# Holding branch a's mask additions in GpSimd's queue until the dilated branch has issued its last addition

## The chip, the cores and the metric

The kernel runs on one core of a Trainium2 chip. The metric is the device time of one execution in microseconds (us), lower is better. The times of the kernel before are the median of three runs.

The engines are named as in the profile: PE (TensorE, matrix products; PEld is its weight loads), DVE (VectorE), ACT (ScalarE), POOL (GpSimd) and SP (SyncE, which only issues transfers here). Each engine works through its own queue of instructions, and the engines wait for each other through semaphores.

## The reference

One decoder layer with 256 tokens and 1024 features. One projection of x feeds three parallel token mixers, whose outputs are gated, merged and normalised; a feed-forward part follows.

```python
proj = x @ w_in[i]
aq, ak, av, iq, ik, iw, bq, bk, bv, cq, ck, cv = jnp.split(proj, SPLIT_POINTS, axis=-1)
o_a = dsa_mixer(...)      # 6 heads: an indexer picks the top 64 keys of each query, softmax over these
o_b = dilated_mixer(...)  # 4 slots, each with 3 query groups of another window and dilation
o_c = moba_mixer(...)     # 6 heads, with 256 tokens: plain causal attention
merged = gates[:, :, 0] * (o_a @ w_br_a) + gates[:, :, 1] * (o_b @ w_br_b) + gates[:, :, 2] * (o_c @ w_br_c)
x = layer_norm(ALPHA * x + merged @ w_out, ln1_g, ln1_b)
h = square(relu(x @ w_up)) @ w_down
x = layer_norm(ALPHA * x + h + sigmoid(x @ w_ple_gate) * (p @ w_ple), ln2_g, ln2_b)
```

Two details matter for the change. In branch b the three query groups of a slot are merged by their softmax denominators; since all three attend to the same keys, this is the sum of their three exponentials divided by the sum of their denominators. In branch a the top-64 choice is a mask that is added to the position bias before the softmax.

## The kernel before

Everything is in fp32. A product is made of three passes on PE, from a high and a low part of each factor (`prod`, lines 133 to 135). So every block of weights that comes from memory (a transfer issued by SP, L71) is split first: ACT casts the high part (`whi`, L75), and the low part (`wlo`, L79) is subtracted by DVE for the first 640 of 1024 columns and by POOL for the rest, up to the 58th block. Five buffers hold raw blocks and five hold split ones. `W.get` splits up to four blocks ahead of the one that PE uses.

The order in each engine's queue is not the order of the program. A planner lays out all queues from its own model of time: among the instructions that are ready in that model it takes the one with the higher priority, mostly the earlier one in the program, so a later instruction that is ready can fill a gap. On the chip each queue then runs in the order that was laid out.

The part around the change, in the program's order:

- **Branch b**, two pairs of slots (`for j in range(2)`, with `slots` for the attention). For each of the two heads of a pair, ACT takes the exponentials of all three groups (L366), POOL adds the second and the third group to the first (L368, then L369, the "query groups" of the change), ACT scales the rows by 1/denominator (`scale_rows`, L333), and in `attend` PE transposes the result (L310 to L312), ACT and DVE split it (L313, L314), and PE multiplies by the values (L317 to L320).
- The features p are loaded and split (`pr`, L466; ACT L467, DVE L468), for use near the end of the layer, and the values of branch c are computed (`values`; copies at L299 and L300).
- **Branch c**, three pairs of heads. The position bias of a head is a tile `T`, loaded by SP from a table in memory (`toeplitz`, L182; three heads to a tile, one transfer each) into one of three buffers.
- **Branch a**, three pairs of heads. The mask `am` (L444) is the result of the top-64 search, a generator called `side` that is advanced step by step from `feat`. For each head n, POOL adds it to the bias tile: `ta = T + am`, in two instructions (L497 for 128 columns, L498 for 256). `ta` has three buffers. DVE reads it in `head` (L341). When the third head of a tile has its `ta`, the buffer of `T` is free for the next tile.

PE works between all of this on gate products (`fill("g")`, results at L238), branch projections (`"c"`, L251) and feature products (`feat`).

An order can be set by hand with `tc.issue_after(ins)`: each instruction traced inside the block on the engine of `ins` is placed behind `ins` in that engine's queue. It is an edge for the planner and adds no semaphore.

Of the kernel before, what the change touches and what calls it, by code (L numbers as in the profile page):

```python
# [13 lines left out]
ALU = mybir.AluOpType  # L14
# [79 lines left out]
def hybrid_layer(ctx: ExitStack, tc: tile.TileContext, x0, xn, pT, wqk, wva, wvb, wg, wbc, wba,  # L94
                 wout, wup, wdq, wdn, wpg, wple, lnrow, rel, onehot, pick, out):
    nc = tc.nc
    pe, act, dve, pool = nc.tensor, nc.scalar, nc.vector, nc.gpsimd
# [69 lines left out]
    for t in TASKS:  # L167
# [4 lines left out]
        elif t in "gcao":  # L172
            u, w, n = {"g": (u_g, wg, 1024), "c": (u_bc, wbc, 640), "a": (u_ba, wba, 768),
                       "o": (u_out, wout, 1024)}[t]
# [4 lines left out]
    def toeplitz(h0, step):  # L179
        t = tp.tile([128, 3, 256], F32, name="T", tag="T")  # L180
        for i in range(3):
            nc.sync.dma_start(t[:, i], bass.AP(  # L182
                tensor=tabd.tensor,
                offset=tabd.offset + (h0 + i * step) * COPIES * N_U + 127,
                ap=[[N_U - 16, 8], [N_U - 1, 16], [1, 256]]))
        return t
# [8 lines left out]
    am = p1.tile([128, 384], F32, name="am")  # L195
# [10 lines left out]
        t = mm.tile([128, 512], F32, name="mm", tag="mm")  # L206
        return t[:, 0:256] if shape == 256 else t

    last = [None]

    def q_pair(ps, scale=-0.125):

        q = qpool.tile([128, 2, S], F32R, name="q", tag="q")
        last[0] = act.mul(q[:, 0], ps, scale).ins
        dve.scalar_tensor_tensor(q[:, 1], ps, scale, q[:, 0].bitcast(F32), op0=ALU.mult,
                                 op1=ALU.subtract)
        return q
# [13 lines left out]
    def fill(what):  # L231


        for w in what:
            if w == "g":
                ps = mmbank(256)
                gemm(ps, u_g[n_g[0]], xs)
                act.activation(G[:, n_g[0]], ps, AF.Tanh, scale=0.5)  # L238
                n_g[0] += 1
                continue  # L240
            f = n_c[0]
            n_c[0] += 1
            hi, lo = W.get(u_bc[f][0])
            ps = mmbank(512).rearrange("p (i s) -> p i s", i=2)
            for i, (k0, k1) in enumerate(((3, 5), (5, 8))):
                for k in range(k0, k1):
                    c = slice((k - 3) * 128, (k - 2) * 128)
                    prod(ps[:, i], (hi[:, c], lo[:, c]), (op[:, k, 0], op[:, k, 1]), k == k0,
                         k == k1 - 1)
            g = G[:, 3 * f + 1:3 * f + 3]  # L250
            dve.scalar_tensor_tensor(g, g, 1.0, ps, op0=ALU.add, op1=ALU.mult)  # L251
            dve.tensor_tensor(g[:, 0], g[:, 0], g[:, 1], op=ALU.add)

    def feat(f):
        ps = mmbank(256)
        gemm(ps, u_q[f], xs)
        if f > 4:
            next(side, None)
        return ps

    def logits(q, k):


        ss = [next(ps_s)[:, 0:384] for _ in range(2)]
        with tc.high_priority(offset=500):
            for b in range(2):
                c = slice(b * 128, (b + 1) * 128)
                for i, (x, y) in enumerate(((1, 0), (0, 0), (0, 1))):
                    for h in (1, 0):
                        d = slice(64 * h, 64 * h + 64)  # L270
                        m = pe.matmul(ss[h][:, QC[b]], lhsT=q[d, x, c],  # L271
                                      rhs=k[d, y, 0:128 * (b + 1)], start=i == 0, stop=i == 2)
                        if b or i or not h:
                            tc.keep_in_program_order(m)
        return ss
# [3 lines left out]
    op = pm.tile([128, 8, 2, S], F32R, name="op")  # L279
# [25 lines left out]
    def attend(P, vh, o, h):  # L305

        hi, lo = pth[n_pt[0] % 2], ptl[n_pt[0] % 2]
        n_pt[0] += 1
        t = next(ps_t)
        pe.transpose(t[:, 0:128], P[:, 256:384], ident)  # L310
        pe.transpose(t[:, 128:256], P[:, 0:128], ident)
        pe.transpose(t[:, 256:384], P[:, 128:256], ident)  # L312
        act.copy(hi[:, 128:512], t[:, 0:384])  # L313
        dve.tensor_tensor(lo[:, 128:512], t[:, 0:384], hi[:, 128:512].bitcast(F32),  # L314
                          op=ALU.subtract)
        v = next(ps_v)
        pe.matmul(v[:, 0:S], lhsT=V[:, 0, vh], rhs=hi[:, 256:512], start=True, stop=False)  # L317
        pe.matmul(v[:, 0:S], lhsT=V[:, 0, vh], rhs=lo[:, 256:512], start=False, stop=False)
        pe.matmul(v[:, 0:S], lhsT=V[:, 1, vh], rhs=hi[:, 0:256], start=False, stop=False)
        pe.matmul(v[:, 0:S], lhsT=V[:, 1, vh], rhs=lo[:, 0:256], start=False, stop=True)  # L320
        x = wk2.tile([64, S], F32, name="ov", tag="ov")
        act.copy(x, v[64:128, 0:S])
        dve.tensor_tensor(o[64 * h:64 * h + 64], v[0:64, 0:S], x, op=ALU.add)

    def pair_out(o, kt):
        act.copy(op[:, kt, 0], o)
        dve.tensor_tensor(op[:, kt, 1], o, op[:, kt, 0].bitcast(F32), op=ALU.subtract)

    def scale_rows(P, den):
        r = sm.tile([128, 2], F32, name="r", tag="r")  # L330
        dve.reciprocal(r, den)
        for b in range(2):
            act.mul(P[:, QC[b]], P[:, QC[b]], r[:, b:b + 1])  # L333


    def head(s, t0, t1, vh, o, h):
        e = wk.tile([128, 384], F32, name="e", tag="e")
        mx = sm.tile([128, 2], F32, name="mx", tag="mx")
        den = sm.tile([128, 2], F32, name="den", tag="den")
        for b, t in enumerate((t0, t1)):  # L340
            dve.tensor_tensor_reduce(e[:, QC[b]], s[h][:, QC[b]], t, op0=ALU.add, op1=ALU.min,  # L341
                                     scale=1.0, scalar=-GONE, accum_out=mx[:, b:b + 1])
        for b in range(2):
            act.activation(e[:, QC[b]], e[:, QC[b]], AF.Exp, bias=mx[:, b:b + 1], scale=-1.0,
                           accum_out=den[:, b:b + 1])
        scale_rows(e, den)
        attend(e, vh, o, h)

    def slots(qs, k, Ts, vh, o):

        es = [wk2.tile([128, 3, 384], F32, name="eb", tag="eb") for _ in range(2)]
        mxs = [sm.tile([128, 2, 3], F32, name="mxb", tag="mxb") for _ in range(2)]
        for g in range(3):
            s = logits(qs[g], k)
            for h in range(2):
                for b, t in enumerate((Ts[h][:, g, 128:256], Ts[h][:, g, :])):
                    dve.tensor_tensor_reduce(es[h][:, g, QC[b]], s[h][:, QC[b]], t, op0=ALU.add,
                                             op1=ALU.min, scale=1.0, scalar=-GONE,
                                             accum_out=mxs[h][:, b, g:g + 1])
        for h in range(2):  # L360
            e = es[h]
            m = sm.tile([128, 2], F32, name="mx", tag="mx")
            den = sm.tile([128, 2], F32, name="den", tag="den")
            dve.tensor_reduce(m, mxs[h], axis=AX.X, op=ALU.min)
            for b in range(2):
                act.activation(e[:, :, QC[b]], e[:, :, QC[b]], AF.Exp, bias=m[:, b:b + 1],  # L366
                               scale=-1.0, accum_out=den[:, b:b + 1])
            pool.tensor_tensor(e[:, 0], e[:, 0], e[:, 1], op=ALU.add)  # L368
            pool.tensor_tensor(e[:, 0], e[:, 0], e[:, 2], op=ALU.add)  # L369
            scale_rows(e[:, 0], den)  # L370
            attend(e[:, 0], vh + h, o, h)

# [15 lines left out]
    with ExitStack() as begin:  # L388
# [4 lines left out]
        with tc.high_priority(offset=1000):  # L393
            for k in range(KT):
                for i, (a, b) in enumerate(cut[k]):
                    e = nc.scalar if i else nc.sync
# [28 lines left out]
    for j in range(4):  # L425
# [3 lines left out]
        for h in range(2):  # L429
            act.activation(r[:, h], s[h], AF.Relu)  # L430
            for b in range(2):
                n = 2 * j + h
# [15 lines left out]
    def opair():  # L448
        return wk2.tile([128, S], F32, name="o", tag="o")
# [21 lines left out]
    for j in range(3):  # L471
# [5 lines left out]
        for h in range(2):  # L477
            n = 2 * j + h
            if n % 3 == 0:
                T = toeplitz(18 + n, 1)  # L480
            head(s, T[:, n % 3, 128:256], T[:, n % 3], 5 + n, o, h)
            fill("g")
        pair_out(o, 5 + j)

    for _ in side:
        pass
    T = None
    for j in range(3):
        q = q_pair(feat(19 + j))
        s = logits(q, kA)  # L490
        o = opair()
        for h in range(2):
            n = 2 * j + h
            if n % 3 == 0:
                T = toeplitz(n, 1)
            ta = wk.tile([128, 384], F32, name="ta", tag="ta")
            pool.tensor_tensor(ta[:, 0:128], T[:, n % 3, 128:256], am[:, 0:128], op=ALU.add)  # L497
            pool.tensor_tensor(ta[:, 128:384], T[:, n % 3], am[:, 128:384], op=ALU.add)  # L498
            head(s, ta[:, 0:128], ta[:, 128:384], 0, o, h)
            fill("gc")  # L500
        pair_out(o, j)
# [436 lines left out]
```

## Time and profile before

| quantity | value |
|---|---|
| time, median of 3 runs | 444.92 us (444.71 to 445.08) |
| time of the profiled execution | 445.0 us |
| its span, first to last instruction | 443.2 us |
| mean granted PE clock | 0.994 of full speed |
| GpSimd's additions for branch b (L368, L369), both pairs | 8 instructions, 8.6 us |
| GpSimd's mask additions (L497, L498) | 12 instructions, 8.3 us |
| GpSimd's weight subtractions (L79) | 58 instructions, 78.5 us |

The span is what the trace covers; the remaining 1.8 us of the execution lie outside it. A row of the timeline gives start, duration, engine, line, operation, output and inputs with their shapes, and in brackets how long the engine had been idle and what ended that wait. Rows of one line that follow each other may be merged (x2, x3). A row of PE's waits gives who waited for whom, the total, the number of times and the longest one. A row of the table by windows gives a stretch of the span and its length, then for PE, PEld, DVE, ACT and POOL the busy time with the number of instructions, the granted clock, the share of the DMA engines and GB/s.

### The profile page before, as it was taken

To read this page: it belongs to the slowest core of one execution; us is meant where nothing else is said; L and a number is where in the kernel's file an instruction comes from. 1 tells how busy PE (TensorE), PEld (TensorE's weight loads), DVE (VectorE), ACT (ScalarE), POOL (GpSimd) and SP (SyncE) were. 2 spreads that over 40 slices of the span, in tenths; PEclk is the share of its full clock that TensorE was granted. 3 is DMA by queue.
4 is the path that set the end of the run, shared out by engine and by line. 5 is a ranking of instruction groups with operands and counts; after the bars stand their busy time and mean duration, and the time that the engine had idled before them with its cause. 6 is when DMAs were issued, how large, how long until landed. Compare 5 with 4: busy or idle time off the path is not lost.

```text
span 443.2 us, 7744 instructions
## 1 busy us (share of the span) xinstructions
PE 429.7 (97%) x2839; PEld 389.3 (88%) x2839; DVE 333.7 (75%) x601; ACT 270.7 (61%) x488; POOL 102.8 (23%) x99
## 2 busy tenths in 40 slices
PE   8999999998999999999999999999999999999992
PEld 8989999998999989999886888888888888888882
DVE  5867977536546568759958769999888978689956
ACT  6765366476877758756604657878877765455500
POOL 2764247378533545500001000000000000000001
PEclk9999999999999999999999999999999999999997
DMA  8895956448635326468870766567655364656502
GB/s 302 298 314 156 286 160 199 150 113 281 224 94 170 126 77 184 131 202 315 260 283 0 248 226 193 190 191 270 204 189 184 100 207 132 228 195 212 215 0 95
DMA packets 27146, 84.28 MB, mean 190 GB/s; under 512 B 2864, under 2 KB 6872, under 8 KB 26724
## 3 DMA queue, kind: packets, MB, share of 16 engines
q1 hardware_dynamic: 25872, 79.54, 54.4%
q10 hardware_dynamic: 1140, 4.19, 2.6%
q8 instruction: 22, 0.36, 0.3%
q14 instruction: 16, 0.13, 0.1%
q0 software_dynamic: 96, 0.06, 0.0%
HBM read 81.88 MB, written 1.90 MB: 189 GB/s over the span
## 4 chain that ended last, share of the span: by engine, by line
PE 89%; DVE 3%; issue 2%; DMA 2%; POOL 2%; ACT 1%; SPq 0%; POOLq 0%; DVEq 0%
PE mm L681 13%; PE mm L133 12%; PE mm L135 12%; PE mm L134 12%; PE b L133 8%; PE b L135 8%; PE b L134 8%; PE mm L683 7%; PE b L271 3%; PE b L409 3%; DMA T<-tabd 1%; DMA pr<-in_pT_dram 1%; PE b L129 1%; DVE st L605 1%; DVE Y L622 1%
## 5 line engine op out<-in xcount | busy, mean ns | idle before, releaser
L75 ACT CAST whi<-raw 128x1024 fp32r<-128x1024 f32 (+3 forms) x147 | 148.0, 1013 | 81.2 <-issue 19.9
L79 DVE TENSOR_TENSOR wlo<-raw,whi 128x1024 fp32r<-128x1024 f32 (+5 forms) x147 | 156.1, 1076 | 42.7 <-ACT whi L75 38.7
L79 POOL TENSOR_TENSOR wlo<-raw,whi 128x384 fp32r<-128x384 f32 (+3 forms) x58 | 78.5, 1359 | 83.2 <-ACT whi L75 74.0
L133 PE MATMUL mm<-xh,whi 128*128 128x256 f32 x336 | 95.0, 283 | 1.0 <-DVE G L251 1.0
L135 PE MATMUL mm<-xh,wlo 128*128 128x256 f32 x336 | 95.6, 285 | 0.0
L134 PE MATMUL mm<-xl,whi 128*128 128x256 f32 x336 | 94.7, 282 | 0.0
L133 PEld LDWEIGHTS mm<-xh,whi 128*128 128x128 f32 x336 | 63.3, 189 | 1.5 <-DVE G L251 1.2
L681 PE MATMUL mm<-x,whi 128*128 128x512 f32 x256 | 64.1, 392 | 0.0
L135 PEld LDWEIGHTS mm<-xh,wlo 128*128 128x128 f32 x336 | 63.3, 188 | 0.8
L134 PEld LDWEIGHTS mm<-xl,whi 128*128 128x128 f32 x336 | 63.3, 188 | 0.3
L612 POOL TENSOR_TENSOR rs<-rs,half 128x1 f32<-128x1 f32 x4 | 4.1, 1028 | 244.5 <-DVE rs L611 244.5
L681 PEld LDWEIGHTS mm<-x,whi 128*128 128x128 f32 x256 | 46.1, 189 | 8.3
L683 PEld LDWEIGHTS mm<-x,wlo 128*128 128x128 f32 x256 | 34.9, 190 | 2.5
L683 PE MATMUL mm<-x,wlo 128*128 128x256 f32 x256 | 35.7, 282 | 0.0
L134 PE MATMUL b<-wlo,hT 128*128 128x512 f32 (+1 forms) x88 | 33.4, 380 | 0.0
L135 PE MATMUL b<-whi,hT 128*128 128x512 f32 (+1 forms) x88 | 33.4, 379 | 0.0
L133 PE MATMUL b<-whi,hT 128*128 128x512 f32 (+1 forms) x88 | 31.9, 379 | 0.0
L686 DVE TENSOR_REDUCE r<-mm 128x256 f32<-128x512 f32 x32 | 22.0, 687 | 6.0 <-PE mm L683 6.0
L742 DVE TENSOR_TENSOR raw<-raw 128x1024 f32<-128x1024 f32 x12 | 14.7, 1222 | 9.0 <-DMA raw<-in_wdq_dram 9.0
L133 PEld LDWEIGHTS b<-whi,hT 128*128 128x128 f32 x88 | 16.6, 188 | 3.1
L135 PEld LDWEIGHTS b<-whi,hT 128*128 128x128 f32 x88 | 16.5, 188 | 3.2
L134 PEld LDWEIGHTS b<-wlo,hT 128*128 128x128 f32 x88 | 16.5, 188 | 3.1
(194 smaller groups left out, 782.0 us busy)
## 6 DMA issues: line engine op xcount, KB each, us to landing
raw<-in_wup_dram SPq DMA_DIRECT2D x32, 512.0 KB
raw<-in_wg_dram SPq DMA_DIRECT2D x24, 512.0 KB
raw<-in_wdn_dram SPq DMA_DIRECT2D x20, 512.0 KB
raw<-in_wqk_dram SPq DMA_DIRECT2D x18, 512.0 KB
raw<-in_wdq_dram SPq DMA_DIRECT2D x12, 512.0 KB
raw<-in_wout_dram SPq DMA_DIRECT2D x8, 512.0 KB
raw<-in_wpg_dram SPq DMA_DIRECT2D x8, 512.0 KB
T<-tabd SPq DMA_DIRECT2D x24, 128.0 KB
```

The lines of the kernel that those rows point to most:

```text
L75: nc.scalar.copy(hi, r)
L79: e.tensor_tensor(lo[:, c], r[:, c], hi[:, c].bitcast(F32), op=ALU.subtract)
L129: pe.transpose(t[:, 0:128], ident, ident)
L133: pe.matmul(ps, lhsT=a[0], rhs=b[0], start=first, stop=False)
L134: pe.matmul(ps, lhsT=a[0], rhs=b[1], start=False, stop=False)
L135: pe.matmul(ps, lhsT=a[1], rhs=b[0], start=False, stop=last)
L271: m = pe.matmul(ss[h][:, QC[b]], lhsT=q[d, x, c], rhs=k[d, y, 0:128 * (b + 1)], start=i == 0, stop=i == 2)
L409: pe.matmul(first[f], lhsT=w[:, k, 128 * f:128 * f + 128], rhs=x[:, k], start=k == i == 0, stop=k == KT - 1 and i == 2)
L681: pe.matmul(ps, lhsT=hi[:, cs[k]], rhs=x1[:, :, k], start=k == 0, stop=False)
L683: pe.matmul(ps[:, :, 0], lhsT=lo[:, cs[k]], rhs=x1[:, :, k, 0], start=False, stop=k == KT - 1)
L686: dve.tensor_reduce(r, ps.rearrange("p b a t -> p b t a"), axis=AX.X, op=ALU.add)
L742: dve.tensor_tensor(t[n], t[x], t[y], op=ALU.subtract)
```

## The change

The last L369 that the program traces (second pair, second head) is remembered, and the mask additions of all six heads of branch a are traced inside an `issue_after` block behind it. `toeplitz`, which loads the bias tiles, and `head`, which reads `ta`, stay outside the block.

```diff
-    last = [None]
+    last, added = [None], [None]
...
             pool.tensor_tensor(e[:, 0], e[:, 0], e[:, 1], op=ALU.add)
-            pool.tensor_tensor(e[:, 0], e[:, 0], e[:, 2], op=ALU.add)
+            added[0] = pool.tensor_tensor(e[:, 0], e[:, 0], e[:, 2], op=ALU.add).ins
...
-    T = None
+    T, held = None, added[0]
...
             ta = wk.tile([128, 384], F32, name="ta", tag="ta")
-            pool.tensor_tensor(ta[:, 0:128], T[:, n % 3, 128:256], am[:, 0:128], op=ALU.add)
-            pool.tensor_tensor(ta[:, 128:384], T[:, n % 3], am[:, 128:384], op=ALU.add)
+            with tc.issue_after(held):
+                pool.tensor_tensor(ta[:, 0:128], T[:, n % 3, 128:256], am[:, 0:128], op=ALU.add)
+                pool.tensor_tensor(ta[:, 128:384], T[:, n % 3], am[:, 128:384], op=ALU.add)
```

The computation is the same. The planner lays out the queues anew with these edges.

## The prediction

> **What bounds the kernel now.** The page comes first: the engine totals.
>
> ```profile
> span 443.2 us, 7744 instructions
> PE 429.7 (97%) x2839; PEld 389.3 (88%) x2839; DVE 333.7 (75%) x601; ACT 270.7 (61%) x488; POOL 102.8 (23%) x99
> ```
>
> PE is busy for all but 13.5 us. A change on POOL, an engine with 23%, can pay only where POOL makes PE wait. So the second view is the list of PE's waits, and the third the table by windows, to place them.
>
> ```profile
> PE b L310 <- POOL wlo L79: 1.4, 1, 1.4
> PE mm L133 <- DVE G L251: 1.0, 1, 1.0
> PE b L310 <- issue: 0.8, 1, 0.8
> ...
> 61.00:73.00 12.00, 12.00 (x108) 11.85 (x107) 7.73 (x16) 9.78 (x21) 9.83 (x9) 1.00 0.50 150
> 82.00:98.00 16.00, 15.32 (x111) 14.86 (x109) 6.16 (x17) 9.25 (x18) 9.26 (x10) 1.00 0.51 149
> 98.00:107.00 9.00, 7.56 (x62) 7.30 (x63) 4.92 (x6) 5.42 (x10) 8.19 (x9) 1.00 0.66 205
> 107.00:150.00 43.00, 43.00 (x377) 42.08 (x377) 25.07 (x66) 32.16 (x79) 20.39 (x14) 1.00 0.53 168
> 150.00:190.00 40.00, 38.98 (x341) 38.10 (x340) 28.82 (x72) 28.41 (x71) 21.15 (x20) 1.00 0.46 139
> ```
>
> After the stretch, PE's busy time and the share of each other engine follow, then the granted clock (1.00 everywhere here). Around the second dilated pair PE loses 16.00 − 15.32 = 0.68 and 9.00 − 7.56 = 1.44 us, 2.12 in all: the two waits before L310, the first transpose of a head's weights. The third wait, 1.0 us, lies in the window from 150 us, after the held additions of the first three heads. Between, PE is gapless.
>
> The fourth view is POOL's timeline around the two waits.
>
> ```profile
> 89.53 1.02 POOL L368 TENSOR_TENSOR eb<-eb 128x384 f32<-128x384 f32 x1
> 92.73 0.47 POOL L497 TENSOR_TENSOR ta<-T,am 128x128 f32<-128x128 f32 x1 [2.19 <-DMA T<-tabd]
> 93.16 1.32 POOL L498 TENSOR_TENSOR ta<-T,am 128x256 f32<-128x256 f32 x1
> 94.44 1.04 POOL L497 TENSOR_TENSOR ta<-T,am 128x128 f32<-128x128 f32 x1
> 95.44 0.73 POOL L498 TENSOR_TENSOR ta<-T,am 128x256 f32<-128x256 f32 x1
> 96.13 1.01 POOL L369 TENSOR_TENSOR eb<-eb 128x384 f32<-128x384 f32 x1
> ...
> 98.06 1.01 POOL L79 TENSOR_TENSOR wlo<-raw,whi 128x384 fp32r<-128x384 f32 x1
> 99.02 0.47 POOL L497 TENSOR_TENSOR ta<-T,am 128x128 f32<-128x128 f32 x1
> 99.45 0.74 POOL L498 TENSOR_TENSOR ta<-T,am 128x256 f32<-128x256 f32 x1
> 100.14 3.16 POOL L79 TENSOR_TENSOR wlo<-raw,whi 128x384 fp32r<-128x384 f32 x2
> 103.27 1.00 POOL L369 TENSOR_TENSOR eb<-eb 128x384 f32<-128x384 f32 x1
> ```
>
> POOL does L368 of head 0 and then waits 2.19 us for a bias tile of branch a, does four mask additions that nobody needs yet, and only at 96.13 the second addition of the same head. Head 1's second addition comes at 103.27, behind a third pair of mask additions and three weight subtractions (L79).
>
> The fifth view follows both heads through ACT and PE, the sixth is SP's queue.
>
> ```profile
> 90.88 3.14 ACT L75 CAST whi<-raw 128x1024 fp32r<-128x1024 f32 x3
> 97.17 0.80 ACT L333 ACTIVATE eb<-eb,r 128x128 f32<-128x128 f32 x2 [3.15 <-POOL eb L369]
> 104.86 0.62 ACT L467 CAST ph<-pr 128x512 fp32r<-128x512 f32 x1 [3.58 <-DMA pr<-in_pT_dram]
> 105.39 0.80 ACT L333 ACTIVATE eb<-eb,r 128x128 f32<-128x128 f32 x2
> ...
> 97.05 0.27 PE L134 MATMUL mm<-xl,whi 128*128 128x256 f32 x1
> 98.08 0.30 PE L310 MATMUL b<-ident,eb 128*128 128x128 f32 x1 [0.75 <-issue]
> 104.65 0.28 PE L134 MATMUL mm<-xl,whi 128*128 128x256 f32 x1
> 106.28 0.30 PE L310 MATMUL b<-ident,eb 128*128 128x128 f32 x1 [1.36 <-POOL wlo L79]
> ...
> 100.22 0.60 SPq L182 DMA_DIRECT2D T<-tabd  x1
> 100.92 0.39 SPq L466 DMA_DIRECT2D pr<-in_pT_dram  x1
> ```
>
> Head 0: L369 ends 97.14, ACT's two scalings (L333) end 97.97, PE's transpose starts 98.08, though PE was free at 97.32. Head 1: L369 ends 104.27, but ACT was not waiting for it: L467 stands ahead of L333 in ACT's queue and waits for the transfer of pr. L333 ends 106.19, the transpose starts 106.28. The row blames an L79 that ended at the same moment; ACT's scaling is what L310 reads. And pr was issued late because SP's queue had first to issue a T at 100.22, whose buffer came free when the third mask addition ended at 99.45 + 0.74 = 100.19. So the first wait is POOL's directly, the second a chain: mask addition, T, pr, ACT, PE.
>
> **The change, part by part.** No instruction is added or removed. The twelve mask additions (six at L497, six at L498) get an order within POOL's queue, no semaphore. Heads 3 to 5 of branch a already run after 150 us; only heads 0 to 2, six additions, move, from 92.73–100.19 to behind L369 of head 1. The planner lays out all queues again with that edge in it.
>
> *Head 0.* L369 follows L368: 89.53 + 1.02, start 90.6, end 91.6, instead of 97.14. If ACT keeps its three casts ahead, they end at 90.88 + 3.14 = 94.02, L333 at 94.82, and the transpose can start 0.11 later, 94.9. PE comes there at 97.32, with 2.4 us to spare. The 0.75 us go. Next late is PE itself.
>
> *Head 1.* L368 can start at 91.6 (ACT has finished the exponentials when it turns to its casts at 90.88). If all three L79 come before L369 at 1.66 us each (the longer row below), L369 starts at 97.6 and ends at 98.6. It then reaches ACT ahead of pr, and ACT is idle for 3.58 us before L467, from 101.28. L333 there ends at 102.1, and the transpose can start at 102.2; PE arrives at 104.93 − 0.75 = 104.18. The 1.35 us between 104.93 and 106.28 go too, with 2 us to spare. This needs the planner to put L333 ahead of L467, which it should: its operands no longer come after the additions that precede pr.
>
> *The moved additions.* Their results are first read much later:
>
> ```profile
> L341 DVE CUSTOM_DVE_ANT_0 e<-b,ta x12: 276/351/421, 150.7 to 182.8; 128x128 f32<-128x128 f32 x6, 128x256 f32<-128x256 f32 x6
> ```
>
> so 45 us cover them. Queued behind them on POOL are weight subtractions, and waiting for the T buffer they free is SP's queue: a T, then pr, then weight loads. POOL's backlog from 89.53 is four additions at 1.02, three L79 at 1.66 and three pairs of mask additions at 0.47 + 0.74 = 1.21: 4.1 + 5.0 + 3.6, so the third pair ends at 102.2, 2.0 later than now. If all six take their long form (1.04 and 1.32 above) it is 105.7; if the L79 come after them, 97.2. What a later SP costs the weights is bounded by the next weight transfer in the queue and its use:
>
> ```profile
> 99.09 0.33 SPq L71 DMA_DIRECT2D raw<-in_wqk_dram  x1
> 107.25 1.67 POOL L79 TENSOR_TENSOR wlo<-raw,whi 128x384 fp32r<-128x384 f32 x1 [1.06 <-issue]
> 121.45 0.39 ACT L214 ACTIVATE q<-mm 128x256 fp32r<-128x256 f32 x1
> ```
>
> The weights asked for at 99.09 are split by 108.92 and their product is read out at 121.45, after 24 matmuls (eight blocks, three products). The window from 107 to 150 has 377 matmuls in 43.00 us, 0.114 each, so PE begins with these at about 118.7: an estimated 9.8 us of cover. Against that a T 2.0 to 5.5 us late costs nothing. The load at 99.09 itself waits for the L79 at 98.06, which should now run around 93, so the weights gain some lead.
>
> *Contention.* Two rows show what POOL pays beside DVE:
>
> ```profile
> 109.33 0.83 DVE L79 TENSOR_TENSOR wlo<-raw,whi 128x640 fp32r<-128x640 f32 x1 [0.16 <-issue]
> 109.37 1.66 POOL L79 TENSOR_TENSOR wlo<-raw,whi 128x384 fp32r<-128x384 f32 x1 [0.44 <-ACT whi L75]
> ```
>
> 1.66 us, against 1.01 for the same shape at 98.06: 0.65 more, less than DVE's 0.83. Head 0's L369 falls before DVE's next subtractions, head 1's pair beside them; so the L79 are priced at 1.66, and the additions' long forms above are the same effect. The Trainium skill speaks against the change here: "SBUF — State Buffer", section "SBUF: two separate sides", says that GpSimd and a VectorE operation with two SBUF inputs take a shared port pair as an exclusive lock, the loser blocked for the whole instruction. The trace shows less than the whole (0.65 of 0.83). By that rule, as an estimate with the row's 0.83, the six packed mask additions would lose up to 5.0 us and end at 107.2 instead of 102.2; with 9.8 us of cover the sum would stay as by the rows, and the second rival below would cost 9.1 us of waiting in place of 4.1.
>
> *Sum.* 0.75 + 1.35 = 2.1 us, out of the 443.2 us span. The execution with this profile took 445.0 (1.8 outside the span), the median is 444.92, so the same 2.1 comes off the median: 442.8. Bounds of this term: nothing and 2.1 from these two waits; 3.1 if the 1.0 at L251 falls away too; below nothing by the second rival. I take 2.1, because the first dilated pair is the nearest case: the same code with no mask addition in the way.
>
> ```profile
> 63.28 1.02 POOL L368 TENSOR_TENSOR eb<-eb 128x384 f32<-128x384 f32 x1 [2.09 <-ACT eb L366]
> 64.37 1.02 POOL L369 TENSOR_TENSOR eb<-eb 128x384 f32<-128x384 f32 x1
> 67.88 1.60 POOL L369 TENSOR_TENSOR eb<-eb 128x384 f32<-128x384 f32 x1
> ```
>
> There L369 comes 1.09 and 4.6 us after the first L368, against 6.6 and 13.7 in the second pair, and PE lost nothing (12.00 of 12.00 in the row for 61 to 73).
>
> **Rivals.**
>
> *Only the first wait goes.* ACT keeps L467 ahead of L333 of head 1 and pr comes as late as now. For it: pr, not POOL, held ACT. Against: L369 now precedes the T and pr in the chain. Gain 0.75: 444.2.
>
> *The T buffer holds SP (the slower side).* The third mask addition ends later than 100.19, the T behind it is issued later, pr stands behind that T, and L467 stays ahead of L333. From T to pr is 0.7 us and from pr's issue to L467 3.94; from L467's start to the transpose 1.42. With the additions ending at 102.2 pr goes at 102.9, the transpose at 108.3, and PE, there at 104.18, waits 4.1 instead of 2.1 in all: 446.9; with 105.7 it is 450.4. It decides from the point where pr is issued after 100.92 with that ACT order. For it: POOL's backlog of 12.7 us. Against: it needs a plan that puts the scaling behind a later transfer.
>
> *The new plan moves a wait elsewhere.* The waits of this stage are 0.8 to 1.4 each. One more costs about 1.4: 444.2; two, 445.6. The one at L251 lost instead: 441.8. For it: every queue is laid out afresh, and PE has no other slack. Against: the edge touches six short instructions far from their readers.
>
> *The change does not do it:* the additions are held but L369 still goes behind the three L79 and the T: 444.9.
>
> **How the numbers follow.** Forecast 442.8: 0.48. Only the first wait: 0.13. SP held: 0.11. New plan better 0.08, worse by one wait 0.09, by two 0.06. No effect 0.05. What a measurement of this kernel can tell from no change is about 0.2%, 0.9 us. Faster: 0.48 + 0.08 = 0.56; within: 0.13 + 0.09 + 0.05 = 0.27; slower: 0.11 + 0.06 = 0.17. The range runs from 441.7, just under the better plan, to 446.0, over two new waits; what SP's case gives lies outside it, and some of the odd plans.
>
> **What would show it.** Right: on POOL no L497 between 89 and the last L369; head 0's L369 about 1.1 after its L368; no L310 among PE's waits; both PE windows full; L333 of head 1 before L467 on ACT. Wrong: L467 still ahead of L333; a new row of PE waits on weights (L133 to L135), which would mean the cover of 9.8 us failed; the span's gain unlike the change in PE's idle time between 82 and 190.

## The result, and the profile after

The changed kernel takes 442.26 us (median of 6 runs, 441.70 to 442.39), the kernel before beside it 445.00 (6 runs, 443.44 to 445.37). The ratio is 0.9939, 95% interval 0.9927 to 0.9951: 2.7 us faster. 442.8 was forecast.

PE's list of waits in the changed kernel, whole, and then the table by windows for the stretches shown of before:

```profile
PE b L129 <- POOL ident masks.py:199: 1.6, 1, 1.6
PE mm L133 <- DVE G L251: 1.0, 1, 1.0
PE b L133 <- ACT x L635: 0.5, 2, 0.2
PE b L135 <- DVE x L636: 0.4, 1, 0.4
PE b L381 <- DMA relt<-in_pick_dram: 0.2, 1, 0.2
```

```profile
82.00:98.00 16.00, 16.00 (x119) 15.73 (x118) 9.45 (x20) 12.39 (x24) 12.01 (x12) 1.00 0.66 190
98.00:107.00 9.00, 9.00 (x79) 9.00 (x78) 6.38 (x8) 4.55 (x8) 8.07 (x7) 1.00 0.56 160
```

No L310 waits any more, and both windows are full. The wait at L251 is still there, 1.0 us. Now POOL's timeline:

```profile
88.83 1.02 POOL L368 TENSOR_TENSOR eb<-eb 128x384 f32<-128x384 f32 x1
89.93 1.02 POOL L369 TENSOR_TENSOR eb<-eb 128x384 f32<-128x384 f32 x1
90.91 1.02 POOL L368 TENSOR_TENSOR eb<-eb 128x384 f32<-128x384 f32 x1
91.89 1.60 POOL L79 TENSOR_TENSOR wlo<-raw,whi 128x384 fp32r<-128x384 f32 x1
93.45 1.59 POOL L369 TENSOR_TENSOR eb<-eb 128x384 f32<-128x384 f32 x1
95.00 1.04 POOL L498 TENSOR_TENSOR ta<-T,am 128x128 f32<-128x128 f32 x1
96.01 0.74 POOL L499 TENSOR_TENSOR ta<-T,am 128x256 f32<-128x256 f32 x1
...
98.84 0.74 POOL L499 TENSOR_TENSOR ta<-T,am 128x256 f32<-128x256 f32 x1
99.54 6.53 POOL L79 TENSOR_TENSOR wlo<-raw,whi 128x384 fp32r<-128x384 f32 x5
```

(The mask additions are now L498 and L499.) L369 of head 0 comes 1.10 us after its L368, that of head 1 4.6 us after the first L368, as in the first dilated pair, and POOL no longer idles for T. ACT, PE and SP follow:

```profile
92.08 0.79 ACT L333 ACTIVATE eb<-eb,r 128x128 f32<-128x128 f32 x2
95.08 0.81 ACT L333 ACTIVATE eb<-eb,r 128x128 f32<-128x128 f32 x2 [0.81 <-POOL eb L369]
98.82 0.62 ACT L467 CAST ph<-pr 128x512 fp32r<-128x512 f32 x1
```

```profile
95.77 0.27 PE L310 MATMUL b<-ident,eb 128*128 128x128 f32 x1
100.82 0.27 PE L310 MATMUL b<-ident,eb 128*128 128x128 f32 x1
```

```profile
96.32 0.33 SPq L466 DMA_DIRECT2D pr<-in_pT_dram  x1
99.60 1.24 SPq L182 DMA_DIRECT2D T<-tabd  x2
```

L333 of head 1 stands ahead of L467. Both scalings end 2.9 and 4.9 us before their transposes, which start without a wait. And pr goes 4.6 us earlier than before, 0.7 of it because this run was ahead from its start (next table), now ahead of T.

**Where the time went.** The first traces differ by more than the times: spans 443.2 and 439.9. Both hold 2839 matmuls, so the n-th start of PE in one can be compared with the n-th in the other (worked out from the starts in the traces, counted from 0). The lead is the time by which the changed kernel is ahead:

| matmul | before, us | after, us | lead |
|---|---|---|---|
| 120 | 18.67 | 17.69 | 0.98 |
| 720 | 89.78 | 89.08 | 0.69 |
| 880 | 112.60 | 109.12 | 3.47 |
| 1120 | 140.12 | 136.76 | 3.36 |
| 1520 | 187.45 | 184.13 | 3.33 |
| 2800 | 430.07 | 426.76 | 3.31 |

All that the change does lies between the 720th and the 1120th: 2.67 us (PE's order differs locally, which makes the 880th a little early), and nothing of it is given back later. The 0.69 before that is a faster start of that run: up to the 763rd matmul PE has the same order in both kernels (on the start, see the run "again" and the last section).

### The profile page after: what moved, and what is told of

Its sections match the earlier page's. It is cut to its first block, busy times and chain, and to the rows that moved or that the text cites. A ratio compares the mean times of both kernels' runs of the same rounds, so it can differ in the third digit from the quotient of the medians.

```text
span 439.9 us, 7745 instructions
## 1 busy us (share of the span) xinstructions
PE 428.3 (97%) x2839; PEld 388.3 (88%) x2839; DVE 339.5 (77%) x601; ACT 270.8 (62%) x488; POOL 102.0 (23%) x99
## 4 chain that ended last, share of the span: by engine, by line
PE 88%; DMA 4%; DVE 3%; issue 2%; POOL 1%; ACT 0%; SPq 0%; POOLq 0%; DVEq 0%
PE mm L682 13%; PE mm L133 13%; PE mm L135 13%; PE mm L134 13%; PE b L133 8%; PE b L135 8%; PE b L134 8%; PE mm L684 7%; PE b L271 3%; DMA raw<-in_wva_dram 2%; DMA G<-in_x_dram 1%; DMA relt<-in_pick_dram 1%; POOL wlo L79 1%; PE b L317 1%; DVE st L606 1%
## 5 line engine op out<-in xcount | busy, mean ns | idle before, releaser
L79 DVE TENSOR_TENSOR wlo<-raw,whi 128x1024 fp32r<-128x1024 f32 (+5 forms) x147 | 160.5, 1107 | 42.2 <-ACT whi L75 39.3
L79 POOL TENSOR_TENSOR wlo<-raw,whi 128x384 fp32r<-128x384 f32 (+3 forms) x58 | 77.0, 1336 | 82.8 <-ACT whi L75 70.2
```

What stands on the lines that cost most here:

```text
L79: e.tensor_tensor(lo[:, c], r[:, c], hi[:, c].bitcast(F32), op=ALU.subtract)
```

## The experiments

Each kernel's time is compared with that of the kernel before on the same chip. The last column is PE's lead over the first trace of before, gained between the 720th and the 1100th matmul, from one trace each. It leaves the start of the run out.

| run | median, us | ratio to before (95%) | PE's gain, us |
|---|---|---|---|
| changed kernel | 442.26 | 0.9939 (0.9927 to 0.9951) | 2.67 |
| after_again | 442.24 | 0.9948 (0.9935 to 0.9961) | 2.67 |
| hold_01 | 442.29 | 0.9942 (0.9930 to 0.9954) | 2.63 |
| hold_to_h0 | 443.01 | 0.9953 (0.9936 to 0.9969) | 1.96 |
| t_behind_pr | 444.21 | 0.9990 (0.9980 to 1.0001) | 0.98 |
| pr_copy | 444.40 | 0.9990 (0.9978 to 1.0002) | 0.73 |
| hold_2 | 444.55 | 0.9995 (0.9986 to 1.0003) | 0.72 |
| again (before) | 445.35 | one run | −0.07 |
| late | 442.39 | 0.9938 (0.9914 to 0.9962) | 1.50 |
| gate_first | 442.33 | 0.9948 (0.9932 to 0.9965) | 2.62 |
| gate_edge | 443.92 | 0.9979 (0.9966 to 0.9991) | 2.67 |

### Fewer edges: hold_01

```diff
-            with tc.issue_after(held):
+            with (tc.issue_after(held) if n < 2 else ExitStack()):
```

> Only the mask additions of heads 0 and 1 are held; those of heads 2 to 5 are free. The planner then lays out every queue exactly as in the changed kernel, so this is the change with fewer edges, and a second measurement of it. If PE's two waits are the whole gain, PE's matmuls must be ahead of the kernel before by 2.66 us over the stretch from 89 to 112 us (what the traces show when starts are compared with starts), and the time is 2.7 lower than that of the kernel before, ratio 0.994. Rival, that the gain in the first comparison was partly luck of the start of the run (PE's 40th matmul came 0.98 us earlier there): the ratio comes out nearer 0.9953, 2.1 us.

PE gained 2.63 and the ratio is 0.9942. So the edges on heads 2 to 5 do nothing, those on heads 0 and 1 are the change. Three measurements of the same queues give 0.9939, 0.9942 and 0.9948. The interval of the second excludes no change by far, but its upper end, 0.9954, just reaches 0.9953, so the times alone do not tell 2.1 from 2.7 us; the traces do, 2.63 to 2.67 three times.

### The start of a run: again

> The kernel before once more, for a second trace of it. If the start of a run varies by itself, PE's 120th matmul and its 720th come at other times than in the first trace (18.67 and 89.78 us) by as much as the changed kernels' traces differ there, up to 1.6 us, while the stretch from the 720th to the 880th takes the same time within 0.1 us and shows the same two waits before L310. Rival, that the change itself moved the start: the start agrees with the first trace within 0.1 us.

The 120th matmul came at 18.68, to 0.01 the time of the first trace, as the rival had it there; the 720th came at 90.03, 0.26 later than in the first trace of the same kernel. What decides against the rival are the three traces of the changed kernel's queues (changed kernel, after_again, hold_01): at the 720th they are 0.69 and 0.18 us earlier than the first trace of before and 0.32 later. All traces of this study together lie between 0.75 us earlier and 1.60 later there. Between the 720th and the 1100th the two traces of before agree to 0.07, with 1.0 and 1.2 us at L310 in place of 0.8 and 1.4. The start is a matter of the run, and no effect of the change.

### Only the third head held: hold_2

```diff
-            with tc.issue_after(held):
+            with (tc.issue_after(held) if n == 2 else ExitStack()):
```

> Only head 2's mask additions are held; those of heads 0 and 1 stay between L368 and L369 of the second pair's head 0, with the wait for their T. Theory, that the two waits have two causes: the first wait before L310 stays (about 0.75 in the list of waits, 0.9 from start to start), the second goes, since L369 of head 1 no longer stands behind head 2's additions and L333 of head 1 comes ahead of L467. Time 1.5 to 1.7 us below the kernel before. Rival, that the third mask addition does nothing and all comes from the first four: no gain, both waits stay. Rival, that the additions of heads 0 and 1 are harmless: 2.7 us gained.

PE's two transposes in this kernel:

```profile
98.31 0.30 PE L310 MATMUL b<-ident,eb 128*128 128x128 f32 x1 [1.00 <-POOL eb L369]
104.33 0.30 PE L310 MATMUL b<-ident,eb 128*128 128x128 f32 x1 [0.35 <-issue]
```

The first wait stayed, at 1.00: the first mask addition waited 2.87 us for its T here, against 2.19. The second shrank from 1.36 to 0.35, but did not go: with the mask additions of heads 0 and 1 ahead, POOL comes to head 1's L369 only at 101.80. PE gained 0.72, half of what was expected, and the time hardly shows it: its interval, 0.9986 to 1.0003, does not exclude the first rival's "no gain". In the trace both rivals fall: one wait is left and the other mostly gone.

### Only ACT's order: pr_copy

```diff
-    act.copy(ph, pr)
+    with tc.issue_after(scaled[0]):     # the last L333 of the second pair
+        act.copy(ph, pr)
```

> Nothing is held on POOL; only ACT's copy of pr (L467) is placed behind the last scaling (L333) of the second dilated pair. Theory, that ACT's wait for pr made the second wait: L333 of head 1 starts when L369 ends, at about 104.3 in place of 105.4 us, and the transpose 1.1 us earlier; the first wait stays. Time 1.1 us below the kernel before, and a second wait of 0.3 us is left to POOL. Rival, that the second wait was POOL's subtraction or L369, as its row says: no change, below 0.3 us.

### Only SP's order: t_behind_pr

```diff
-                T = toeplitz(n, 1)
+                with (tc.issue_after(loaded) if n else ExitStack()):   # loaded: the transfer of pr
+                    T = toeplitz(n, 1)
```

> Nothing is held on POOL, and ACT's order is that of the kernel before; only the loads of branch a's second bias tile are placed behind the load of pr in SP's queue. Theory, that pr was late because a T ahead of it waited for the third mask addition: pr is issued at about 99.5 in place of 100.9 us, L467 starts 1.4 us earlier, and the second wait shrinks by about 1.1 us, until L369 at 104.3 is what is late. Time 1.1 us below the kernel before. Rival, that something else delays pr (the bandwidth, the raw weight load ahead of it): pr lands as before, no change.

These two leave POOL's queue as it was. The first pair of rows shows both transposes in pr_copy, the second ACT in t_behind_pr.

```profile
99.76 0.30 PE L310 MATMUL b<-ident,eb 128*128 128x128 f32 x1 [0.84 <-issue]
106.90 0.30 PE L310 MATMUL b<-ident,eb 128*128 128x128 f32 x1 [0.53 <-issue]
```

```profile
102.22 0.62 ACT L467 CAST ph<-pr 128x512 fp32r<-128x512 f32 x1 [1.79 <-DMA pr<-in_pT_dram]
103.46 0.80 ACT L333 ACTIVATE eb<-eb,r 128x128 f32<-128x128 f32 x2 [0.62 <-POOL eb L369]
```

In both the second wait falls from 1.36 to 0.53, and what ACT then waits for is L369 of head 1. So the row of before, which blamed a weight subtraction on POOL, was wrong, and the chain T, pr, L467, L333 was right; but L369 stands close behind it: it ended at 104.27 in the kernel before, 1.1 us ahead of the L333 that pr held up until 105.39. PE gained 0.73 and 0.98 where 1.1 was expected, and the times fell by 0.3 and 0.5 us, with intervals that just touch no change.

### Only head 0's addition ahead: hold_to_h0

```diff
-    T, held = None, added[0]     # the last L369, head 1
+    T, held = None, added[-2]    # the last but one, head 0
```

> The mask additions wait only for L369 of the second pair's head 0, not of head 1, so all six of the first three heads stand between the two heads' additions again; ACT has L467 ahead of L333 of head 1, as in the kernel before, but pr is ahead of T on SP. Theory, that the first wait is POOL's order alone and that pr is late because head 0's transposes, which free its buffer, are late: the first wait goes, pr is issued at about 96 us, and L369 of head 1, at about 103.4 us, leaves 0.3 to 0.5 us of the second wait. Ahead of the kernel before by 1.8 to 2.2 us over the 720th to the 880th matmul. Rival, that only the hold of head 1's addition matters: the second wait stays at 1.4 and 1.0 us is gained.

```profile
96.55 0.27 PE L310 MATMUL b<-ident,eb 128*128 128x128 f32 x1
104.28 0.30 PE L310 MATMUL b<-ident,eb 128*128 128x128 f32 x1 [0.49 <-issue]
```

The first wait is gone, 0.49 of the second is left, and PE gained 1.96; the time fell by 1.85. One thing came otherwise: pr was issued at 99.18, not at 96, because the weight load ahead of it on SP waited 5.8 us for a subtraction (L79) on POOL. So the hold up to head 0's addition brings most of the gain, and the one up to head 1's the last 0.6 to 0.7.

### Held longer: late

```diff
-    T, held = None, added[0]
+    T, held = None, W.low[34]    # the 34th block's L79 on POOL
```

> The changed kernel with the mask additions held some 15 us longer, behind a weight subtraction that runs at about 117 us. Theory, that nobody needs them before about 147 us and that SP's queue has time: as the changed kernel within 0.4 us (442.3), no new wait of PE on weights. Rival, that the T buffer they free holds up the transfers behind it, or the additions then delay the subtractions: PE waits at L133 to L135, 1 us or more slower than the changed kernel.

The mask additions ran from 115.90 to 119.87. The median, 442.39, is that of the changed kernel, so the times of four runs show no cost of 20 us more of delay; their interval is wide, 0.9914 to 0.9962. The trace, of the slowest of the four (443.11), does show one: PE gained 1.50 in place of 2.67, and there is one wait more, at the second head's value product (L318 here):

```profile
107.21 0.36 PE L318 MATMUL b<-pth,V 128*128 128x256 f32 x1 [0.90 <-DVE o L324]
```

SP now had two weight loads ahead of pr, issued it at 98.27, and ACT stood 4.86 us at the cast of pr with the copy that PE needed behind it. So PE had no wait on weights, as expected, and the additions stood in nobody's way; but the new layout put pr later in SP's queue, and ACT's order passed it on. Whether the other three runs have this wait no trace shows.

### The last wait of the stage: gate_first and gate_edge

```diff
+            with tc.high_priority(offset=500):
                 dve.scalar_tensor_tensor(g, g, 1.0, ps, op0=ALU.add, op1=ALU.mult)
```

> The changed kernel, and DVE's first gate product of branch c (L251) is given a higher priority, so that it need not stand behind a weight subtraction. It goes for PE's last wait of this stage, 1.0 us before an L133 near 158 us. If the wait is only a matter of DVE's order, PE gains its 1.0 us and about 0.16 more, since the list counts from the modelled end of a matmul: 441.1. Rival, that the subtraction itself is late (its block was released late) and PE waits for it next: no gain, the wait only changes its name.

The planner kept DVE's order: the wait stayed at 1.0, the time at 442.33. So this run did not test the wait. An edge did:

```diff
-                for ins in self.after:
+                for ins in (self.gate[:1] if self.done == 46 else self.after):   # gate[0]: the first L251
```

> The changed kernel, and DVE's part of one weight subtraction (the 46th block, at 157.4 us in the changed kernel) is placed behind the first gate product of branch c (L251, at 158.2). In the changed kernel that product's inputs are ready from about 153 us, and DVE idles 2.45 us in front of the subtraction, which waits for ACT. Theory, that a DVE order makes PE's last wait of this stage as POOL's order made the other two: the wait at L133 of 1.0 us goes and PE gains 1.0 to 1.2 us: 441.2, ratio to the kernel before 0.9915. Rival, as with the priority: the wait only takes another name, 442.3.

```profile
158.31 0.69 DVE L251 SCALAR_TENSOR_TENSOR G<-G,mm 128x512 f32<-128x512 f32 x1 [2.72 <-PE mm L135]
```

```profile
208.21 0.50 PE L133 MATMUL b<-whi,q 128*128 128x512 f32 x1 [1.41 <-ACT q L573]
```

The product went ahead, and then it waited 2.72 us itself, for PE: its inputs were not ready at 153, as the expectation had it. So DVE's order made only part of the wait: the wait at L251 shrank to 0.5, and PE's lead rose by 0.47. But the queues behind that edge were laid out anew, and near 208 us a new wait of 1.4 appeared, where PE's lead fell by 2.0: from 3.09 at the 1700th matmul to 1.12 at the 1900th, both counted from the 720th. The kernel is 1.7 us slower than the changed one. No kernel here beats the changed one beyond the noise.

### One more measurement: after_again

> The changed kernel once more, on the same chip as the run with the gate product ahead, so that the two can be compared: ratio to the kernel before 0.994, within 0.001 of the two earlier measurements.

0.9948, as expected.

## Why the prediction held, and where it was off

**What bounds it: right.** PE's order of work and its waits set the time; what PE stopped waiting between 82 and 107 us came out at the end unchanged.

**Head 0: right.** L369 was to start 1.1 us after L368 and did. ACT put L333 even ahead of its third cast, and the transposes had 2.8 us to spare where 2.4 were counted.

**Head 1: right in mechanism, with a link missing.** L333 came ahead of L467, and L369 ended earlier than counted: at 95.04, which is 95.7 on the clock of the kernel before, instead of 98.6, with one L79 ahead of it and not three. pr_copy and t_behind_pr show the chain through pr, each from one end. What the prediction did not see is in SP's own list of waits in the changed kernel:

```profile
SPq L182 <- POOL ta L499: 2.8, 1, 2.8
SPq L466 <- PE b L312: 2.4, 1, 2.4
```

pr waits for PE's L312, head 0's last transpose, because its tile takes the buffer of head 0's exponentials. So a late head 0 keeps pr back too. In the kernel before this did not bind: L312 ended at 98.59, and what pr waited for until 100.92 was T. Nor did it in t_behind_pr and hold_to_h0, where a weight load ahead of pr on SP was later. That removing the second wait alone brought only 0.7 to 1.0 has its reason in the rows above: with POOL's order as before, L369 of head 1 is late as well.

**The moved additions: right on the cover, wrong on the contention.** They ended at 99.58 (100.3 on the clock of the kernel before), against 102.2 counted (97.2 to 105.7): 4.6 us for the three pairs, with two of six in the long form. SP stood 2.8 us for the T buffer, with weight loads behind it, and PE did not wait for weights. Here the Trainium skill's rule, an exclusive lock with the loser blocked for the whole instruction ("SBUF — State Buffer", section "SBUF: two separate sides"), was weighed against the rows. The prediction took the 0.65 lost beside a subtraction of 0.83 for less than the rule. But POOL had begun 0.04 after DVE, so only 0.79 of DVE's instruction was left. Three rows of the changed kernel show the same from both sides:

```profile
97.12 0.74 POOL L499 TENSOR_TENSOR ta<-T,am 128x256 f32<-128x256 f32 x1
97.29 1.26 DVE L79 TENSOR_TENSOR wlo<-raw,whi 128x640 fp32r<-128x640 f32 x1 [0.45 <-ACT whi L75]
97.82 1.05 POOL L498 TENSOR_TENSOR ta<-T,am 128x128 f32<-128x128 f32 x1
```

DVE's subtraction, 0.83 alone, began with 0.57 of POOL's addition left and took 0.43 longer. POOL's next addition, 0.47 alone, began with 0.73 of DVE's left and took 0.58 longer. Each lost what was left of the other's instruction, less some 0.14 us; in 41 of the 47 cases in this trace where POOL began an instruction beside such a subtraction it lost that much, less 0.12 to 0.16, and most of the others are of shapes that never run alone there. So these runs agree with the rule. The six did not lose "up to 5.0", because only two of them began beside a subtraction of DVE; they lost 0.57 and 0.58, and L369 0.57 (1.59 against 1.02). The prediction also left out that DVE pays: its subtraction at 101.61 took 1.65 instead of 0.83. It cost PE nothing here.

**The sum: a term was mis-sized.** "0.75 + 1.35 = 2.1 us" should have been 2.67, more than the 2.1 that the prediction gave as the most these two waits could bring; so the forecast of 442.8 lies above all six runs (441.70 to 442.39). The two numbers are what the list of waits gives, from the modelled end of a matmul to the start of the next. But in a gapless stretch matmuls start every 0.12 us, though each is drawn 0.28 long. From start to start the two gaps were 98.08 − 97.05 = 1.03 and 106.28 − 104.65 = 1.63; less 0.12 each they cost 0.91 and 1.51, 2.42 together. The starts in the trace give some 0.2 more: behind the first gap three steps from start to start are 0.20 to 0.22 long, where the changed kernel has one such step. That leaves less than 0.1, which stays open. The page says that matmul ends are modelled. The Trainium skill says it too ("Perfetto Trace Analysis", section "Tensor Engine Instruction"): the reported end is an estimate and no observation. Both could have been used here and were not.

**The rivals.** Only the first wait: no; but where the additions may stand between the two heads' L369, as in hold_to_h0, 0.49 of the second does stay. SP held by T: the T did come after the additions and SP did stand for it, but pr was ahead of both, so the case did not arise; it was not forced in a run, and its price is untested. A new plan moving a wait: not in the changed kernel; gate_edge shows it, 0.5 us gained at one place and 2.0 lost 50 us later, and late shows one of 0.9. No effect of the change: no.

**Open.** In hold_2, pr_copy and t_behind_pr the medians fell by 0.2, 0.3 and 0.5 us where the traces show PE ahead by 0.7 to 1.0. The intervals reach to gains of 0.6, 1.0 and 0.9 us, so much of this can be noise. In t_behind_pr's trace 0.4 of the gain is given back near 395 us, mostly at one product with a weight's low part (0.58 are left at the 2800th matmul), and the same happens in hold_to_h0 (1.56 left); the changed kernel's trace has no such loss. Each trace is one run, so this was not settled. Nor was POOL's order tried by itself: with the edge the planner also put pr ahead of T on SP and L333 ahead of L467 on ACT, and no run has POOL's new order with both of these as before.

## What to carry to other kernels

In a queue that runs in order, an instruction that nobody needs for 50 us can hold up one that is needed at once, and a planner that fills gaps by its own model of time can put it there (presumably when a transfer lands later on the chip than in the model, which no run here shows); the sign is a wait for a transfer in front of it, on an engine that is otherwise far from the bound. Price a wait of PE from start to start, less the pitch of the matmuls around it, and compare two traces by the n-th matmul: that shows where the time came from and takes the luck of the start out. Look at the recorded clock before calling a difference between two runs unexplained. One edge has consequences beyond its place, good ones here and bad ones in gate_edge, so look at the whole of PE's lead, not only at the wait that was meant.

## What was not expected of the hardware

The start of a run varies, with the same instructions in the same order. These rows are of PE in the kernel before and then in the changed one, at the same matmuls:

```profile
6.18 1.05 PE L409 MATMUL b<-xh,sl 128*128 128x256 f32 x4
```

```profile
5.83 0.64 PE L409 MATMUL b<-xh,sl 128*128 128x256 f32 x4
```

Four matmuls took 1.05 us in one run and 0.64 in the other, and 0.98 us had come together by the 120th. The records of the granted clock in the traces show what goes with it. The record of full clock begins at 7.63 us in the kernel before and at 5.36 in the changed one, with no record ahead of it (the table by windows counts what has no record as full, so it shows 1.00 there). Until that time these matmuls start every 0.21 us, after it every 0.12. In the twelve traces the record begins between 4.4 and 7.7 us, and the step changes within 0.1 us of it in ten of them, within 0.5 in the other two. Where it began earliest PE gained little, because it then waited for its inputs: 0.9 us before an L409 in hold_01 (4.38 us).

pr_copy's trace shows the same in the middle. These are windows of pr_copy and then one of the kernel before:

```profile
28.00:30.00 2.00, 2.00 (x15) 1.72 (x14) 0.12 (x1) 1.02 (x4) 0.53 (x1) 0.78 0.92 288
30.00:33.00 3.00, 3.00 (x17) 3.00 (x16) 2.95 (x7) 1.75 (x4) 0.85 (x1) 0.58 0.89 298
```

```profile
30.00:33.00 3.00, 3.00 (x32) 2.85 (x30) 2.79 (x6) 1.82 (x6) 1.01 (x1) 1.00 0.88 300
```

Half the clock is on record there from 29.1 to 32.5 us, and matmuls of this shape again start every 0.21 us; 15 steps lost 1.5 us. PE also stood 0.8 us for the table load (L381), 0.9 from start to start. Together these are the 2.4 us by which its lead went from 0.82 at the 120th matmul to −1.58 at the 300th. So the clock and the landing of the first inputs make most of the luck of the start. That the clock is at half ahead of its first record is inferred from the equal step; what decides when it changes no run here shows.
